# A four-mixer backbone: the closing stage of each layer with the projection kept in PSUM, mask and gate applied apart, block-diagonal scores, one denominator step and folded norm vectors

## The chip, the cores and the metric

The kernel runs on one core of one Trainium2 chip. The metric is device time in microseconds (us) of one execution. Engines are called as in the profile: PE or TensorE (matmul; PEld its weight loads), DVE or VectorE, ACT or ScalarE, POOL or GpSimd, SP or SyncE, which issues all DMAs of this kernel from one queue.

## The reference, cut to what matters

Two layers; 256 context and 2048 latent tokens, width 1024. Each layer projects a normed input, runs four mixers of width 256 (mLSTM, Hyena, GLA, windowed attention), joins their outputs, multiplies by `w_out` and adds the normed, gated result to its input. The change touches the mLSTM's readout, the head norms of mLSTM and GLA, and the joint output projection:

```
# mlstm_chunks, per head
w_intra = exp(d - m);  w_inter = exp(inter - m)          # d is masked to -inf outside the triangle
s   = (q @ k^T) * w_intra
num = w_inter * (q @ c_prev) + s @ v
den = w_inter * (q @ n_prev) + sum(s)
h   = num / max(abs(den), exp(-m))                       # one scan forward, one backward, added
# finish (mLSTM; GLA without the sigmoid)
h = h * sigmoid(o);  h = h * rsqrt(mean_head(h*h) + EPS) * norm_g;  h = h * silu(gate)
# close of the layer
y = concat([a, hyena, gla, attn]) @ w_out[l]
x = x + gt * (y * rsqrt(mean(y*y) + EPS) * g_post)
```

Latent tokens alone are returned, so layer 1 needs no output for the context.

## The kernel before, in words

Tokens are cut into 18 tiles of 128 (2 context, 16 latent). The projections into the mixers run on TensorE as three products of rounded parts (`float32r` high and low), spread between the mixers' own work by marks. The outputs of Hyena, GLA and attention are left, transposed, in the DRAM tensor `aT`.

`tail` (line 1605) closes a layer. It loads `w_out` in 16 blocks of 128x512 through the tile `raw`, a ring of two buffers that all weight loads share: ScalarE rounds a block (`hi`, line 1617), POOL makes the rest (`lo`, line 1618). Then it runs two kinds of generators in turn over the tiles (18 in layer 0, 16 in layer 1), `mlstm_chunk` of tile T and `out_tile` of tile T - 1, with two of them open at a time.

`mlstm_chunk` (line 777) loads the chunk's `aT` part, `qk`, `v`, the states `cb`, the gates `og` and, for each half `m` of two heads, `E`: the row of maxima `m_M` broadcast to 128 partitions. The scores go to the PSUM tile `psA` (two banks), one product of 64 rows for each head (line 801). VectorE subtracts the gate and applies the mask in one instruction for each direction and head (line 804, eight a chunk); ScalarE takes the Exp (line 806); VectorE multiplies with the scores (line 808). `pi` (line 810) is q times the state, `po` (line 816) the weighted values; both stand in PSUM banks `psb` and `psc`. VectorE scales and adds them into `nd` (lines 812, 818), and makes the denominator `r` (lines 821 to 823) and the quotient (line 824) for each half; POOL adds the directions (line 825). `head_norm` (line 657) norms the heads and multiplies by the norm vector `ngb` on POOL (line 665). TensorE transposes the result (line 834, bank `pse`), and it becomes k = 0, 1 of the eight parts of tile T.

`out_tile` (line 1626) rounds the eight parts (line 1638 on ScalarE, line 1639 on POOL) and multiplies them with `w_out` in two halves of 512 columns: 24 matmuls a half (lines 1650 to 1652), k = 2 to 7 first, 0 and 1 last. The sums stand in the PSUM tag `pp`, two banks. VectorE copies a bank to `y` (line 1653), ScalarE squares it in place and sums (line 1654), the small norm steps follow on VectorE and ScalarE, VectorE scales the 1024 columns (line 1659), POOL adds them to `x` (line 1660), and SP stores the tile. In layer 0 six of the tiles are then followed by the input norm of a tile for layer 1 (`norm_tile`, lines 360 to 380, with transposes on TensorE, line 370).

The order of instructions on each engine isn't the order of the code: the framework orders them by a simulated timeline when it builds the program. On the chip each engine runs its list in order, and each tile's buffers tie the engines together by semaphores.

## Time and profile before

| what | us |
|---|---|
| median of 3 runs | 3533.69 |
| lowest, highest | 3526.88, 3543.3 |
| the profiled execution | 3536.89 |
| its span in the profile | 3535.1 |

The profile is of one execution. A time in a timeline counts from the start of its span. Busy time of an engine leaves out its waits on semaphores, but an instruction that is held up after its start counts as busy; matmuls overlap, so the sum of their durations is more than their busy time. The two tails lie at about 1533 to 1883 us (layer 0) and 3228 to 3535 us (layer 1).

### The profile page before, as it was taken

Reading aid. Unit: us, or ns where it says so; the run is one execution under the profiler, and the core shown is the slowest. Engines: PE = TensorE matmul, PEld = TensorE weight load, DVE = VectorE, ACT = ScalarE, POOL = GpSimd, SP = SyncE. Lnnn points to the kernel's source line nnn. Section 1 sums busy time; section 2 is a strip of 40 time slices with the busy share of each in tenths; the row PEclk is TensorE's granted clock in tenths of the full one; section 3 lists DMA queues with packets and bytes.
Section 4 is the critical chain, followed back from the end, with each engine's and each line's share of the span. In section 5 each row is a group of like instructions: output and inputs, shape, how many; then the busy total and the mean of one; then the engine's idle time right before and its main releaser. Section 6 shows DMA issues by size and latency. Waiting matters only on the chain. (4 is left out here: it accounts for less than half of the span.)

```text
span 3535.1 us, 70724 instructions
## 1 busy us (share of the span) xinstructions
PE 3226.2 (91%) x25897; PEld 2653.8 (75%) x25897; DVE 2046.1 (58%) x5374; ACT 1434.5 (41%) x3722; POOL 1153.3 (33%) x1559
## 2 busy tenths in 40 slices
PE   6989999999998988888998899998999999887998
PEld 4778878798886677777777677776888887776776
DVE  6733565553345565568888534656432457745887
ACT  5513444332544444133444323444333546522433
POOL 3711111233123344145555420112231135422555
PEclk8999999999998989989999899999999999998999
DMA  7374443684355532475444365443863443327453
GB/s 248 105 203 125 116 117 101 186 247 130 111 167 155 149 111 82 120 203 176 154 138 137 97 178 156 118 116 118 242 185 97 123 119 105 101 84 210 152 162 106
DMA packets 554861, 508.24 MB, mean 144 GB/s; under 512 B 114896, under 2 KB 484877, under 8 KB 554515
## 3 DMA queue, kind: packets, MB, share of 16 engines
q1 hardware_dynamic: 554515, 503.73, 48.3%
q8 instruction: 205, 3.36, 0.4%
q14 instruction: 141, 1.16, 0.1%
HBM read 337.64 MB, written 165.92 MB: 142 GB/s over the span
## 5 line engine op out<-in xcount | busy, mean ns | idle before, releaser
L480 PE MATMUL pp<-w,hi 128*128 128x256 f32 (+2 forms) x1984 | 602.8, 305 | 23.6 <-ACT w L425 10.4
L482 PE MATMUL pp<-w,hi 128*128 128x256 f32 (+2 forms) x1984 | 595.6, 301 | 4.5 <-POOL w L426 4.5
L483 PE MATMUL pp<-w,ho 128*128 128x256 f32 (+2 forms) x1984 | 590.8, 298 | 5.1 <-POOL ho L380 5.0
L463 PE MATMUL pp<-hi,w 128*128 128x512 f32 (+1 forms) x1328 | 527.0, 397 | 6.5 <-ACT w L425 5.2
L466 PE MATMUL pp<-hi,w 128*128 128x512 f32 (+1 forms) x1328 | 513.6, 389 | 1.2 <-POOL w L426 1.0
L465 PE MATMUL pp<-ho,w 128*128 128x512 f32 (+1 forms) x1328 | 513.6, 387 | 0.0
L480 PEld LDWEIGHTS pp<-w,hi 128*128 128x128 f32 x1984 | 389.3, 197 | 46.4 <-ACT w L425 13.9
L482 PEld LDWEIGHTS pp<-w,hi 128*128 128x128 f32 x1984 | 390.5, 197 | 17.4 <-issue 8.6
L483 PEld LDWEIGHTS pp<-w,ho 128*128 128x128 f32 x1984 | 391.0, 197 | 16.4 <-issue 7.5
L426 POOL TENSOR_TENSOR w<-raw,w 128x256 fp32r<-128x256 f32 (+2 forms) x256 | 194.1, 775 | 554.0 <-ACT w L425 519.2
L463 PEld LDWEIGHTS pp<-hi,w 128*128 128x128 f32 x1328 | 255.9, 193 | 61.0 <-issue 7.3
L466 PEld LDWEIGHTS pp<-hi,w 128*128 128x128 f32 x1328 | 251.8, 191 | 53.2 <-issue 3.9
L465 PEld LDWEIGHTS pp<-ho,w 128*128 128x128 f32 x1328 | 253.6, 191 | 44.1 <-issue 3.0
L1650 PE MATMUL pp<-woh,w 128*128 128x512 f32 x544 | 235.5, 433 | 19.2 <-ACT pp L1654 9.0
L1651 PE MATMUL pp<-wol,w 128*128 128x512 f32 x544 | 223.4, 411 | 0.0
L1652 PE MATMUL pp<-woh,w 128*128 128x512 f32 x544 | 219.2, 412 | 2.0 <-POOL w L1639 2.0
L1010 ACT COPY M<-X 128x512 f32<-128x512 f32 x204 | 128.9, 632 | 181.5 <-DVE X L1034 73.3
L216 DVE COPY st<-pp 128x256 f32<-128x256 f32 (+2 forms) x152 | 79.6, 524 | 205.2 <-PE pp L483 106.1
L218 ACT COPY st<-pp 128x256 f32<-128x256 f32 (+2 forms) x152 | 68.7, 452 | 262.0 <-PE pp L483 140.9
L1032 DVE TENSOR_TENSOR X<-X,A 128x256 f32<-128x256 f32 x204 | 109.4, 536 | 94.8 <-ACT M L1010 92.6
L425 ACT CAST w<-raw 128x256 fp32r<-128x256 f32 (+2 forms) x256 | 96.9, 407 | 158.1 <-DMA raw<-in_w_in_dram 96.7
L1219 POOL TENSOR_TENSOR sg<-sg,gt 128x256 f32<-128x256 f32 x34 | 24.9, 733 | 393.8 <-ACT sg L654 324.8
(589 smaller groups left out, 6932.2 us busy)
## 6 DMA issues: line engine op xcount, KB each, us to landing
raw<-in_w_in_dram SPq DMA_DIRECT2D x96, 256.0 KB
q<-d_tq SPq DMA_DIRECT2D x68, 256.0 KB
E<-d_mM SPq DMA_DIRECT2D x68, 256.0 KB
d_yraw<-st SPq DMA_DIRECT2D x64, 256.0 KB
raw<-in_w_ada_dram SPq DMA_DIRECT2D x64, 256.0 KB
X<-d_gqk SPq DMA_DIRECT2D x102, 128.0 KB
wsho<-d_aT SPq DMA_DIRECT2D x34, 384.0 KB
kl<-d_tk SPq DMA_DIRECT2D x28, 384.0 KB
```

The lines of the kernel that those rows point to most:

```text
L426: nc.gpsimd.tensor_sub(out=t[:, 1, :n], in0=raw[:, i, :n], in1=t[:, 0, :n])
L463: mm = nc.tensor.matmul(out=ps[:, :n], lhsT=a, rhs=hi[:, k], start=(k == 0), stop=False)
L465: nc.tensor.matmul(out=ps[:, :n], lhsT=a, rhs=lo[:, k], start=False, stop=False)
L466: nc.tensor.matmul(out=ps[:, :n], lhsT=b, rhs=hi[:, k], start=False, stop=(k == KD - 1))
L480: mm = nc.tensor.matmul(out=ps[:, :n], lhsT=a, rhs=wk[k][:, 0, :n], start=(k == 0), stop=False)
L482: nc.tensor.matmul(out=ps[:, :n], lhsT=a, rhs=wk[k][:, 1, :n], start=False, stop=False)
L483: nc.tensor.matmul(out=ps[:, :n], lhsT=b, rhs=wk[k][:, 0, :n], start=False, stop=(k == KD - 1))
L1010: nc.scalar.copy(out=grid(M, 0, (cc, 2), (x, 512 // x), (1, cc)), in_=grid(X, 0, (512 + cc, 2), (x, 512 // x), (1, cc)))
L1032: nc.vector.tensor_mul(out=t, in0=t, in1=grid(A, f + 2 * b + 1, (-2 * b - 1, 2), (2, b), (0, cc)))
L1650: nc.tensor.matmul(out=ps, lhsT=ak[k][:, 0], rhs=hi[:, k], start=(k == order[0]), stop=False)
L1651: nc.tensor.matmul(out=ps, lhsT=ak[k][:, 0], rhs=lo[:, k], start=False, stop=False)
L1652: nc.tensor.matmul(out=ps, lhsT=ak[k][:, 1], rhs=hi[:, k], start=False, stop=(k == order[-1]))
```

## The change

- **Projection.** A half's sums stay in their PSUM bank: ScalarE squares out of the bank into `y` as scratch, and VectorE scales straight from the bank after the norm, 512 columns at a time; POOL adds 512 columns at a time. Every third half uses a new bank `psd`, which is free because `psA` now takes one bank.
- **Mask and gate.** VectorE adds the mask to all of `E` (128x512) in one instruction; the gate becomes the bias of the Exp, which therefore runs once for each direction and head.
- **Scores.** One product of 128 rows and 256 columns for a half: `qb` holds q of two heads on the block diagonal, zeros elsewhere (cleared once on POOL, two buffers). It is loaded by two more DMAs a chunk.
- **Denominator.** `nd` holds both halves; `r` is made once a chunk, and POOL adds the directions once.
- **Norm vectors.** `head_norm` no longer multiplies by `ngb`, in mLSTM and in GLA. Instead ScalarE scales the blocks k = 0, 1, 4, 5 of `w_out` by the norm vectors (16 more passes in both layers), which are loaded as columns.

```
--- before.py
+++ after.py
@@ -654,7 +654,7 @@
         nc.scalar.activation(out=s, in_=s, func=ACTF.Exp, scale=-1.0)
         return s
 
-    def head_norm(self, p, h, ngb):
+    def head_norm(self, p, h):
         nc = self.nc
         sq = p.tile([P, 4, 64], F32, tag="so", name="sq", bufs=1)
         ss = p.tile([P, 4], F32, tag="hns", name="ss")
@@ -662,7 +662,6 @@
         nc.vector.reduce_sum(out=ss, in_=sq, axis=AX.X)
         self.rsqrt_mean(p, ss, 64, "hn")
         nc.vector.tensor_mul(out=h, in0=h, in1=ss.unsqueeze(2).to_broadcast([P, 4, 64]))
-        nc.gpsimd.tensor_mul(out=h, in0=h, in1=ngb)
 
     def rounds(self, gens, depth, lead):
         gens = iter(gens)
@@ -767,20 +766,23 @@
                 self.m_S = self.states(p, "m", 65, self.m_qk, self.m_v, weigh, lambda d, c, m: ac[:, d, c, m:m + 1], "cd", (3, 1))
 
     def mlstm_setup(self, l, p):
-        ngb = p.tile([P, 4, 64], F32, name="ngb", bufs=1)
-        self.bcast(ngb.rearrange("p h d -> p (h d)"), self.a["mlstm_norm_g"][l], 256)
         cb = [p.tile([P, 2, 2, 2, 65], F32, name=f"cb{i}", bufs=1) for i in range(2)]
-        for t in cb:
+        qb = [p.tile([P, 2, 2, P], F32, name=f"qb{i}", bufs=1) for i in range(2)]
+        for t in cb + qb:
             self.nc.gpsimd.memset(t, 0.0)
-        return cb, ngb
+        return cb, qb
 
     def mlstm_chunk(self, p, c, shared, ar):
         nc = self.nc
         g, wi, em, ws, ac = self.tabs
-        cbt, ngb = shared[0][c % 2], shared[1]
+        cbt, qbt = shared[0][c % 2], shared[1][c % 2]
         nc.sync.dma_start(out=ar[:, 2:], in_=self.aT[c, :, 2:])
         qk = p.tile([P, 4, P], F32, tag="qk", name="qk")
-        nc.sync.dma_start(out=qk, in_=self.qk_src(self.m_qk, c))
+        src = self.qk_src(self.m_qk, c)
+        nc.sync.dma_start(out=qk, in_=src)
+        for h in range(2):
+            r = slice(64 * h, 64 * h + 64)
+            nc.sync.dma_start(out=qbt[r, :, h], in_=src[r, :2])
         v = p.tile([P, 4, 65], F32, tag="v", name="v")
         nc.sync.dma_start(out=v.rearrange("p h d -> p (h d)"), in_=self.m_v[c])
         for h in range(2):
@@ -792,41 +794,40 @@
         s = self.sigm(p, og, 512, "sg", 2)
         nc.gpsimd.tensor_mul(out=s[:, 256:], in0=s[:, 256:], in1=og[:, 256:])
         yield
-        pS = self.ps("A", (P, 2, 512))
+        pS = self.ps("A", (P, 2, 2, P))
+        nd = p.tile([P, 2, 2, 2, 65], F32, tag="nd", name="nd")
         for m in range(2):
             E = p.tile([P, 2, 2, P], F32, tag="E", name="E", bufs=4)
             nc.sync.dma_start(out=E, in_=self.m_M[c, :, 2 * m:2 * m + 2].rearrange("(o d) h t -> o d h t", o=1).broadcast_to([P, 2, 2, P]))
-            for h in range(2):
-                r = slice(64 * h, 64 * h + 64)
-                nc.tensor.matmul(out=pS[:, h, m * P:m * P + P], lhsT=qk[r, 2 + m], rhs=qk[r, m], start=True, stop=True)
+            nc.tensor.matmul(out=pS[:, m], lhsT=qk[:, 2 + m], rhs=qbt[:, m], start=True, stop=True)
+            nc.vector.tensor_add(out=E, in0=E, in1=self.mbig.unsqueeze(2).to_broadcast([P, 2, 2, P]))
             for d in range(2):
                 for h in range(2):
-                    nc.vector.scalar_tensor_tensor(out=E[:, d, h], in0=E[:, d, h], scalar=g[:, d, c, 2 * m + h:2 * m + h + 1],
-                                                   in1=self.mbig[:, d], op0=ALU.subtract, op1=ALU.max)
-            nc.scalar.activation(out=E, in_=E, func=ACTF.Exp, scale=-1.0)
+                    nc.scalar.activation(out=E[:, d, h], in_=E[:, d, h], func=ACTF.Exp, scale=-1.0, bias=g[:, d, c, 2 * m + h:2 * m + h + 1])
             yield
-            nc.vector.tensor_mul(out=E, in0=E, in1=pS[:, :, m * P:m * P + P].unsqueeze(1).to_broadcast([P, 2, 2, P]))
+            nc.vector.tensor_mul(out=E, in0=E, in1=pS[:, m].unsqueeze(1).to_broadcast([P, 2, 2, P]))
             pi = self.ps(T_I[m], (P, 2, 2, 65))
             nc.tensor.matmul(out=pi, lhsT=qk[:, m], rhs=cbt[:, :, m], start=True, stop=True)
-            nd = p.tile([P, 2, 2, 65], F32, tag="nd", name="nd", bufs=3)
-            nc.vector.tensor_mul(out=nd, in0=pi, in1=wi[:, c, :, 2 * m:2 * m + 2].unsqueeze(3).to_broadcast([P, 2, 2, 65]))
+            nc.vector.tensor_mul(out=nd[:, m], in0=pi, in1=wi[:, c, :, 2 * m:2 * m + 2].unsqueeze(3).to_broadcast([P, 2, 2, 65]))
             po = self.ps(T_O[m], (P, 2, 2, 65))
             for d in range(2):
                 for h in range(2):
                     nc.tensor.matmul(out=po[:, d, h], lhsT=E[:, d, h], rhs=v[:, 2 * m + h], start=True, stop=True)
             yield
-            nc.vector.tensor_add(out=nd, in0=nd, in1=po)
-            r = p.tile([P, 2, 2], F32, tag="r", name="r")
-            den = nd[:, :, :, 64]
-            nc.vector.scalar_tensor_tensor(out=r, in0=den, scalar=-1.0, in1=den, op0=ALU.mult, op1=ALU.max)
-            nc.vector.tensor_max(out=r, in0=r, in1=em[:, c, :, 2 * m:2 * m + 2])
-            nc.vector.reciprocal(out=r, in_=r)
-            nc.vector.tensor_mul(out=nd[:, :, :, :64], in0=nd[:, :, :, :64], in1=r.unsqueeze(3).to_broadcast([P, 2, 2, 64]))
-            nc.gpsimd.tensor_add(out=hh[:, 2 * m:2 * m + 2], in0=nd[:, 0, :, :64], in1=nd[:, 1, :, :64])
+            nc.vector.tensor_add(out=nd[:, m], in0=nd[:, m], in1=po)
             yield
+        r = p.tile([P, 2, 2, 2], F32, tag="r", name="r")
+        den = nd[:, :, :, :, 64]
+        nc.vector.scalar_tensor_tensor(out=r, in0=den, scalar=-1.0, in1=den, op0=ALU.mult, op1=ALU.max)
+        nc.vector.tensor_max(out=r, in0=r, in1=em[:, c].rearrange("p d (m h) -> p m d h", m=2))
+        nc.vector.reciprocal(out=r, in_=r)
+        for m in range(2):
+            nc.vector.tensor_mul(out=nd[:, m, :, :, :64], in0=nd[:, m, :, :, :64], in1=r[:, m].unsqueeze(3).to_broadcast([P, 2, 2, 64]))
+        nc.gpsimd.tensor_add(out=hh.rearrange("p (m h) d -> p m h d", m=2), in0=nd[:, :, 0, :, :64], in1=nd[:, :, 1, :, :64])
+        yield
         hf = hh.rearrange("p h d -> p (h d)")
         nc.vector.tensor_mul(out=hf, in0=hf, in1=s[:, :256])
-        self.head_norm(p, hh, ngb)
+        self.head_norm(p, hh)
         nc.gpsimd.tensor_mul(out=hf, in0=hf, in1=s[:, 256:])
         yield
         ps = self.ps(T_E)
...
     def gla_mix(self, l):
-            ngb = p.tile([P, 4, 64], F32, name="ngb", bufs=1)
-            self.bcast(ngb.rearrange("p h d -> p (h d)"), self.a["gla_norm_g"][l], 256)
...
@@ -1606,6 +1605,9 @@
         nc, a = self.nc, self.a
         last = l == DEPTH - 1
         tiles = list(range(NCT if last else 0, NT))
+        gn = self.gp.tile([P, 4], F32, tag="gn", name="gn")
+        for i, nm in enumerate(("mlstm_norm_g", "gla_norm_g")):
+            nc.sync.dma_start(out=gn[:, 2 * i:2 * i + 2], in_=a[nm][l].rearrange("(k p) -> p k", p=P))
         W = []
         for half in range(2):
             hi = self.hp.tile([P, KD, 512], F32R, tag="hi", name="woh", bufs=4)
@@ -1614,9 +1616,12 @@
             for k in range(KD):
                 raw = self.raw()[:, :, :256]
                 nc.sync.dma_start(out=raw, in_=a["w_out"][l, k * P:(k + 1) * P, 512 * half:512 * half + 512].rearrange("p (i n) -> p i n", i=2))
+                if k in (0, 1, 4, 5):
+                    nc.scalar.activation(out=raw, in_=raw, func=ACTF.Copy, scale=gn[:, (0, 1, 4, 5).index(k):(0, 1, 4, 5).index(k) + 1])
                 nc.scalar.copy(out=hi[:, k].rearrange("p (i n) -> p i n", i=2), in_=raw)
                 nc.gpsimd.tensor_sub(out=lo[:, k].rearrange("p (i n) -> p i n", i=2), in0=raw, in1=hi[:, k].rearrange("p (i n) -> p i n", i=2))
         self.h = {}
+        self.no = 0
         ws = [self.hp.tile([P, 4, D], F32, tag=t, name="ws" + t, bufs=4) for t in ("hi", "ho")]
         with self.banks(f"tl{l}"), self.pool(f"tl{l}") as p:
             shared = self.mlstm_setup(l, p)
@@ -1642,22 +1647,26 @@
                 yield
                 y = ws[0][:, 3]
                 ss = p.tile([P, 2], F32, tag="ss", name="ss")
+                acc = []
                 for half in range(2):
                     hi, lo = W[half]
                     sl = slice(512 * half, 512 * half + 512)
-                    ps = self.psp.tile([P, 512], F32, tag="pp", name="pp")
+                    self.no += 1
+                    ps = self.psp.tile([P, 512], F32, tag="pp", name="pp") if self.no % 3 else self.ps("d")
+                    acc.append(ps)
                     for k in order:
                         nc.tensor.matmul(out=ps, lhsT=ak[k][:, 0], rhs=hi[:, k], start=(k == order[0]), stop=False)
                         nc.tensor.matmul(out=ps, lhsT=ak[k][:, 0], rhs=lo[:, k], start=False, stop=False)
                         nc.tensor.matmul(out=ps, lhsT=ak[k][:, 1], rhs=hi[:, k], start=False, stop=(k == order[-1]))
-                    nc.vector.tensor_copy(out=y[:, sl], in_=ps)
-                    nc.scalar.activation(out=ps, in_=ps, func=ACTF.Square, accum_out=ss[:, half:half + 1])
+                    nc.scalar.activation(out=y[:, sl], in_=ps, func=ACTF.Square, accum_out=ss[:, half:half + 1])
                     yield
                 rs = p.tile([P, 1], F32, tag="rs", name="rs")
                 nc.vector.tensor_add(out=rs, in0=ss[:, 0:1], in1=ss[:, 1:2])
                 self.rsqrt_mean(p, rs, D, "o")
-                nc.vector.scalar_tensor_tensor(out=y, in0=y, scalar=rs, in1=gb, op0=ALU.mult, op1=ALU.mult)
-                nc.gpsimd.tensor_add(out=x, in0=x, in1=y)
+                for half in range(2):
+                    sl = slice(512 * half, 512 * half + 512)
+                    nc.vector.scalar_tensor_tensor(out=y[:, sl], in0=acc[half], scalar=rs, in1=gb[:, sl], op0=ALU.mult, op1=ALU.mult)
+                    nc.gpsimd.tensor_add(out=x[:, sl], in0=x[:, sl], in1=y[:, sl])
                 nc.sync.dma_start(out=dst(T), in_=x)
                 yield
                 if not last and T in NS:
```

How this moves instructions, as built. SP at the start of layer 1's tail, from the first chunk's `qk` on (`cb` and `qb` are the two buffers of each):

```order
L783 DMA qk<-d_mqk 128x4x128
L785 DMA v<-d_mv 128x260
L788 DMA cb_36627<-d_mS 64x4x65 x2
L790 DMA og<-d_mog 128x512
L798 DMA E<-d_mM 128x2x256 x2
L783 DMA qk<-d_mqk 128x4x128
L785 DMA v<-d_mv 128x260
L788 DMA cb_36628<-d_mS 64x4x65 x2
L790 DMA og<-d_mog 128x512
L798 DMA E<-d_mM 128x2x256 x2
```

and with the change:

```order
L782 DMA qk<-d_mqk 128x4x128
L787 DMA v<-d_mv 128x260
L790 DMA cb_36485<-d_mS 64x4x65
L785 DMA qb_36487<-d_mqk 64x2x128 x2
L790 DMA cb_36485<-d_mS 64x4x65
L792 DMA og<-d_mog 128x512
L801 DMA E<-d_mM 128x2x256 x2
L782 DMA qk<-d_mqk 128x4x128
L785 DMA qb_36488<-d_mqk 64x2x128 x2
L787 DMA v<-d_mv 128x260
L790 DMA cb_36486<-d_mS 64x4x65 x2
```

`ngb`, which stood ahead of the first `qk`, is gone; each chunk has its two `qb` loads among its loads, ahead of `og` and `E`. VectorE in layer 1's steady part, over the small norm steps of an output tile (`rs`, 128x1) and those of a chunk (`ss`, 128x4):

```order
L229 TENSOR_TENSOR t<-t,v 128x4
L823 RECIPROCAL r<-r 128x4
L230 SCALAR_TENSOR_TENSOR ss<-t,ss 128x4
L824 TENSOR_TENSOR nd<-nd,r 128x4x64
L804 SCALAR_TENSOR_TENSOR E<-E,G,mbig 128x128
L664 TENSOR_TENSOR hh<-hh,ss 128x256
L804 SCALAR_TENSOR_TENSOR E<-E,G,mbig 128x128 x2
L228 SCALAR_TENSOR_TENSOR t<-rs 128x1
L804 SCALAR_TENSOR_TENSOR E<-E,G,mbig 128x128
L229 TENSOR_TENSOR t<-t,v 128x1
L230 SCALAR_TENSOR_TENSOR rs<-t,rs 128x1
L1659 SCALAR_TENSOR_TENSOR wshi<-wshi,rs 128x1024
```

and with the change:

```order
L225 TENSOR_SCALAR v<-rs 128x1
L664 TENSOR_TENSOR hh<-hh,ss 128x256
L808 TENSOR_TENSOR E<-E,psA 128x512
L228 SCALAR_TENSOR_TENSOR t<-rs 128x1
L229 TENSOR_TENSOR t<-t,v 128x1
L651 TENSOR_SCALAR sg<-og 128x512
L230 SCALAR_TENSOR_TENSOR rs<-t,rs 128x1
L803 TENSOR_TENSOR E<-E,mbig 128x512
L1668 SCALAR_TENSOR_TENSOR wshi<-pp,rs,wshi 128x512
L1668 SCALAR_TENSOR_TENSOR wshi<-psd,rs,wshi 128x512
```

The masking of four blocks is one addition (`E<-E,mbig`), and the scaling of 1024 columns out of `wshi` is two of 512 out of two banks. TensorE in layer 1's steady part, at the scores of a half:

```order
L1652 MATMUL pp<-woh,w 128x512
L816 MATMUL psb<-v,E 128x65 x4
L801 MATMUL psA<-qk 128x128 x2
L1650 MATMUL pp<-woh,w 128x512
L1651 MATMUL pp<-wol,w 128x512
```

and with the change:

```order
L1660 MATMUL pp<-woh,w 128x512
L815 MATMUL psb<-v,E 128x65 x4
L802 MATMUL psA<-qb_36488,qk 128x256
L1658 MATMUL psd<-woh,w 128x512
L1659 MATMUL psd<-wol,w 128x512
```

The scores of a half were two products (one for each head) and are one of twice the columns; the output matmuls behind them, which all went to `pp`, go to `psd` for every third half.

## Rows read from the trace of the kernel before

**Rows 1.** Page: busy us of each engine (share of span), instructions.
```profile
PE 3226.2 (91%) x25897; PEld 2653.8 (75%) x25897; DVE 2046.1 (58%) x5374; ACT 1434.5 (41%) x3722; POOL 1153.3 (33%) x1559
```

**Rows 2.** Stretches: length, busy us (instructions) by engine, clock, DMA share, GB/s.
```profile
1533.00:1580.00 47.00, 38.43 (x166) 29.38 (x165) 37.55 (x110) 17.97 (x38) 18.58 (x25) 0.73 0.81 241
1580.00:1883.00 303.00, 276.05 (x1294) 218.74 (x1293) 259.06 (x637) 118.09 (x327) 170.99 (x184) 0.93 0.46 144
3228.00:3285.00 57.00, 40.79 (x164) 30.73 (x163) 31.16 (x105) 14.52 (x30) 15.55 (x25) 0.64 0.69 173
3285.00:3510.00 225.00, 212.93 (x1041) 167.44 (x1040) 194.14 (x490) 86.80 (x232) 125.54 (x149) 0.98 0.49 150
```

**Rows 3.** Waits of TensorE, layer 0, 1580 to 1883: us in total, times, longest.
```profile
PE pp L1650 <- ACT pp L1654: 5.8, 5, 2.5
PE pp L1650 <- ACT w L1638: 5.3, 3, 2.6
PE psb L810 <- DVE nd L818: 5.0, 2, 4.1
PE psc L810 <- DMA cb<-d_mS: 3.0, 1, 3.0
```

**Rows 4.** By line, same stretch: names, shapes, count; busy us, mean ns; idle before.
```profile
L804 DVE SCALAR_TENSOR_TENSOR E<-E,G,mbig 128x128 f32<-128x128 f32 x104 | 44.9, 481 | 3.2 <-DMA E<-d_mM 3.2
...
L1659 DVE SCALAR_TENSOR_TENSOR wshi<-wshi,rs 128x1024 f32<-128x1024 f32 x17 | 24.6, 1450 | 0.4
L1653 DVE COPY wshi<-pp 128x512 f32<-128x512 f32 x34 | 23.0, 681 | 5.7 <-PE pp L1652 3.1 <-POOL wshi L1660 2.3 <-POOL w L426 0.3
...
L808 DVE TENSOR_TENSOR E<-E,psA 128x512 f32<-128x512 f32 x29 | 19.6, 677 | 1.8 <-PE psA L801 1.8
L1654 ACT ACTIVATE pp<-pp 128x512 f32<-128x512 f32 x33 | 19.2, 582 | 44.0 <-DVE wshi L1653 43.9
L821 DVE SCALAR_TENSOR_TENSOR r<-nd 128x4 f32<-128x4 f32 x30 | 17.3, 576 | 0.1
...
L806 ACT ACTIVATE E<-E 128x512 f32<-128x512 f32 x26 | 16.4, 632 | 52.8 <-DVE E L804 45.6 <-issue 2.3 <-PE pp L1652 1.9
```

**Rows 5.** Waits of TensorE, layer 1, 3285 to 3510.
```profile
PE psb L816 <- DVE E L808: 6.6, 7, 1.8
```

**Rows 6.** Timeline, VectorE, layer 1's filling: start us, us, names, count [idle before].
```profile
3263.20 1.14 DVE L804 SCALAR_TENSOR_TENSOR E<-E,G,mbig 128x128 f32<-128x128 f32 x4 [1.71 <-DMA E<-d_mM]
```

**Rows 7.** Timeline of ScalarE, ahead of layer 1's tail.
```profile
3163.69 0.42 ACT L646 ACTIVATE G<-t 128x72 f32<-128x72 f32 x2
```

**Rows 8.** Timeline near the end: a tile's last matmuls, and its scaling.
```profile
3510.75 0.39 PE L1651 MATMUL pp<-wol,w 128*128 128x512 f32 x1
...
3510.98 0.40 PE L1652 MATMUL pp<-woh,w 128*128 128x512 f32 x1
...
3515.07 1.85 DVE L1659 SCALAR_TENSOR_TENSOR wshi<-wshi,rs 128x1024 f32<-128x1024 f32 x1
```

**Rows 9.** Timeline of TensorE, layer 1's steady part: state products and scores.
```profile
3453.42 0.60 PE L810 MATMUL psb<-cb,qk 128*128 128x260 f32 x2
...
3459.26 0.49 PE L801 MATMUL psA<-qk 64*128 64x128 f32 x4
```

**Rows 10.** Timelines, ScalarE, POOL, SP issues: staging of w_out; a chunk's first load.
```profile
3194.34 0.62 ACT L1617 CAST woh<-raw 128x512 fp32r<-128x512 f32 x1 [2.14 <-DMA raw<-in_w_out_dram]
...
3195.04 1.27 POOL L1618 TENSOR_TENSOR wol<-raw,woh 128x512 fp32r<-128x512 f32 x1 [1.75 <-ACT woh L1617]
...
3196.33 0.37 SPq L1616 DMA_DIRECT2D raw<-in_w_out_dram  x1
...
3240.61 0.57 SPq L783 DMA_DIRECT2D qk<-d_mqk  x1
```

**Rows 11.** Timelines, ScalarE, VectorE, layer 0: Square and scaling of one tile.
```profile
1609.02 0.58 ACT L1654 ACTIVATE pp<-pp 128x512 f32<-128x512 f32 x1 [3.01 <-DVE wshi L1653]
...
1616.24 1.74 DVE L1659 SCALAR_TENSOR_TENSOR wshi<-wshi,rs 128x1024 f32<-128x1024 f32 x1
```

83 lines of the change are left out of this document (46 added, 37 removed).

## The prediction

> **What bounds the kernel now.** I read the page first: TensorE is busy 91% of the span and VectorE 58% [rows 1], so VectorE as a whole bounds nothing. The change is almost all inside `tail`, which runs twice, and an average over the span says nothing about it. So next I cut both tails into a filling part, in which the mLSTM chunks run with hardly any projection beside them, and a steady part, in which one chunk and one output tile pass per turn [rows 2]. In the steady parts VectorE is busy 259 of 303 us (layer 0) and 194 of 225 us (layer 1), 85% and 86%, and TensorE 276 and 213. So TensorE is still the engine nearest to full. It loses two things: idle time, 303 - 276 = 27 us and 225 - 213 = 12 us, and clock. The granted clock is 0.93 and 0.98 there, so 0.07 x 276 = 19 us and 0.02 x 213 = 4 us are lost to stretches at 1.2 instead of 2.4 GHz; in the filling parts it is 0.73 and 0.64. Idle and clock together are 62 us, and no relief of another engine can give back more than that in these stretches.
>
> Then I read what TensorE waits for there. In layer 0 the largest wait is for a projection bank (5.8 us), then a transposed and cast chunk (5.3), then VectorE's `nd` (5.0), then a DMA (3.0) [rows 3]. The bank comes late because ScalarE's Square waits for VectorE's copy out of the same bank: 43.9 of the 44.0 us that ScalarE sat idle before line 1654 are put down to line 1653 [rows 4]. In layer 1 the largest wait is for VectorE's `E` product, 6.6 us [rows 5]. Named directly, VectorE ends 5.8 + 5.0 + 6.6 = 17 of the 39 us idle, 45%. The 5.3 us end with a chain (head norm, transpose, copy, cast) that has VectorE steps in it too.
>
> **The change part by part: VectorE in the steady parts.** I count layer 0, stretch 1580 to 1883 [rows 4]. Removed: the masking instructions of line 804, 44.9 us for 104; the two copies a tile, 23.0 us for 34; the 1024-wide scaling of line 1659, 24.6 us for 17; half of the denominator instructions, of which I count line 821 alone, 17.3 / 2 = 8.7 us. Sum 101 us. Added: 26 additions of 128x512 (104 / 4) and 34 scalings of 128x512 out of PSUM. Line 808 is the nearest row for both, 512 columns, one operand in PSUM, 677 ns. For the scalings I take it: 34 x 0.677 = 23 us. The additions have both operands in SBUF, like line 804, and line 804 is stretched: 481 ns on average, against 1.14 / 4 = 285 ns where nothing else ran [rows 6], a factor 1.7. So an addition costs 0.68 to 1.14 us, 18 to 30 us in all. Relief: 101 - 23 - (18 to 30) = 48 to 60 us of 259; VectorE falls from 85% to some 67%. These are sums of durations that overlap a little, so an estimate. Layer 1 has 11 chunks in its stretch where layer 0 has 13: some 40 to 51 of 194.
>
> What of this reaches the end is bounded by the 62 us above. The releasers name VectorE for 45%; with a part of the cast chain I take a half, 31 us. The low end is 10 (the in-order queues then wait for the next thing, `E`'s DMA above all), the high end 55 (all but the DMA wait and some clock).
>
> **ScalarE.** Eight Exps of 128 columns replace two of 512. The nearest rows: two of 72 columns take 0.42 us [rows 7], one of 512 columns 632 ns [rows 4]. So an Exp of 128 columns lies between 0.21 and 0.63 us, nearest to the first; along the line between them it is 0.21 + 56 x 0.42 / 440 = 0.26. That makes 8 x 0.26 = 2.1 against 1.3 us, 0.8 us more a chunk. ScalarE is busy 118 of 303 us, 39% [rows 2]; it hides this. Without that cover it is 34 chunks x 0.8 = 27 us.
>
> **The bank that is held.** A projection bank is now freed only after Square, norm and scaling; in return there are three banks. In layer 1, where little stands in the queues, the last matmul of a tile starts at 3510.98 and the scaling at 3515.07 [rows 8]. Without the copy (0.68) and with the first scaling (0.68) the first bank is free 4.1 us after that matmul starts. The new order of TensorE puts at least 18 projection matmuls (the first half of the next tile) and a group of mLSTM matmuls in front of the first matmul that needs that bank: 18 x 0.23 (spacing in [rows 8]) = 4.1, plus 0.5 for the scores [rows 9] and as much again for the rest, so 5 us at the least, but for the last tile, and about 7 in the middle. Cost taken: nothing. If the cover is gone, see the second rival.
>
> **Scores on TensorE.** Four instructions on 64 rows (two heads) become two on 128 rows, 256 columns, with zeros in the other head's half. The four take 0.49 us; two instructions on 128 rows with 260 columns take 0.60 [rows 9]. So a chunk half costs 0 to 0.11 us more; 68 of them, 0 to 7 us; I take 0, since the columns streamed are equal (2 x 128). The four 64-row instructions follow each other; nothing shows two of them at once. The Trainium skill says otherwise ("TensorE: Matmul & The Clock Gate", Part 3: Packing small matmuls): products on different row groups overlap in the array. If they had, the pair would have cost about a half and this edit would add 68 x 0.25 = 17 us, for a sum of 3527; since the row prices the pair as it runs here, I give that no chance.
>
> **The filling parts.** Each chunk has two more loads on SP's queue, and `qb` must be cleared by POOL first. SP spends 0.57 us on such an issue there [rows 10], so before the second chunk's `E` loads stand four more, 2.2 us, less the norm vector's load that goes. Behind them on SP are the chunk's `v`, `cb`, `og` and `E`, and VectorE waits for `E` in just this place (1.71 us, [rows 6]). VectorE's shorter masking gives some of it back. I take +2 us a layer, +4; ends -3 and +6.
>
> **The staging of w_out.** Eight of sixteen blocks a layer get one more ScalarE pass of 0.62 us (that of the cast, [rows 10]) in a ring of two buffers. A load of `raw` goes out at 3196.33, just after POOL released the buffer at 3195.04 + 1.27 = 3196.31 [rows 10]: the ring paces SP, and the loads of the state updates stand behind it. Four passes a buffer make 4 x 0.62 = 2.5 us a layer; I take +2, +4 in all, ends 0 and +6. The norm vectors' own small loads come earlier and are hidden.
>
> **The rest.** The last tile saves a copy (0.68) and half a scaling before its store: -1 us. POOL loses 34 products of 256 columns in the GLA mix, and the scheduler reorders other stages too; taken as 0, within 5 us either way.
>
> **Sum.** 3536.9 (profiled execution) - 31 + 4 + 4 - 1 = 3512.9. That execution was 3.2 us above the median 3533.7, so 3509.7, rounded 3510 us.
>
> **The rivals.** First: VectorE was not what held TensorE. For it speaks that TensorE is busy 91 and 95% of the steady parts, that VectorE itself waits for `E`'s DMA [rows 4, 6], and that the first wait it stops ending will be ended by that DMA or by the cast chain. Then nothing comes back and the costs stay: 3533.7 + 7 = 3541 us, no change.
>
> Second, the one on the slow side: the held bank. In layer 0, where the norm of the next layer's tiles stands in the same queues, Square started at 1609.02 and the scaling at 1616.24 [rows 11], 7.2 us; with 0.4 for the last matmul and 0.68 for the scaling the bank would come free after 8.3 us, against a cover of 5 to 8. If most of layer 0's 18 tiles look so, each waits some 1.5 us, and some 1 us more goes to the low clock that follows idle time: 18 x 2.5 = 45 us, 3510 + 45 = 3555 us. It decides as soon as the chain from Square to scaling is above some 7 us on average. Against it: the copy leaves the chain and VectorE's queue gets a fifth shorter.
>
> Third: the whole of it comes back, idle and clock, because each wait that goes also saves a low-clock stretch behind it: 3510 - 24 = 3486 us.
>
> **How the numbers follow.** The forecast has 0.50 (its own range 3496 to 3524), no gain 0.22 (3530 to 3545), the held bank 0.13 (3550 and above), the full gain 0.15 (3480 to 3496). A range of 8 in 10 leaves out the held bank and the edge of the full gain: 3484 to 3545. About 0.5%, 17.7 us, can be told from no change, so faster means below 3516: three quarters of the forecast and the full gain, 0.53; slower the held bank, 0.13; the same 0.34.
>
> **What would show it.** Steady parts of some 285 and 217 us in place of 303 and 225, VectorE under 70% busy there, a granted clock of 0.96 or more in layer 0. The wait for the bank now ends in VectorE's scaling; over 10 us in total for it would prove the second rival. If TensorE's idle time stays at 39 us with VectorE at 67%, the first rival is right. Filling parts longer by over 6 us, or a stretch from the first `w_out` load to the first chunk longer by over 6, would show that I priced the loads too low. I would be wrong altogether if stages outside both tails moved by more than 10 us through the scheduler's new order.

## The result and the profile after

The changed kernel takes 3486.7 us (median; 3483.8 to 3488.9) beside 3535.7 of the kernel before on the same chip: a ratio of 0.986, interval 0.984 to 0.989, so 49 us faster. The forecast was 3510, range 3484 to 3545. Page of after, busy us of each engine, share of the span, instructions (as [rows 1]):

```profile
PE 3193.5 (92%) x25761; PEld 2638.8 (76%) x25761; DVE 1926.2 (55%) x5034; ACT 1473.6 (42%) x3942; POOL 1102.1 (32%) x1495
```

From here on one cut serves for all kernels: *filling* is from the start of the first output matmul to the start of the Square of tile 0's second half, *steady* from there to the start of the last output matmul, and both together are a *tail*. Before, filling and steady take 45.2 and 302.8 us in layer 0, 56.5 and 239.0 in layer 1 (the prediction's cut ended layer 1 at 3510). Views by stretch, first before (steady parts alone), then after (filling, steady, filling, steady); columns as in [rows 2]:

```profile
1579.00:1882.00 303.00, 276.69 (x1296) 219.54 (x1294) 259.03 (x639) 118.40 (x328) 170.14 (x183) 0.93 0.46 144
3285.00:3524.00 239.00, 225.41 (x1094) 177.00 (x1093) 199.73 (x505) 89.66 (x242) 130.31 (x153) 0.99 0.47 145
```

```profile
1545.00:1587.00 42.00, 34.85 (x134) 26.16 (x133) 25.02 (x60) 21.67 (x59) 16.84 (x19) 0.72 0.90 265
1587.00:1865.00 278.00, 256.88 (x1252) 209.13 (x1251) 208.89 (x507) 134.88 (x420) 159.16 (x175) 0.99 0.54 168
3198.00:3252.00 54.00, 42.76 (x139) 31.94 (x140) 27.65 (x68) 20.37 (x60) 12.34 (x18) 0.62 0.66 176
3252.00:3475.00 223.00, 215.99 (x1045) 176.84 (x1045) 151.28 (x383) 99.76 (x309) 120.46 (x141) 1.00 0.52 161
```

VectorE falls from 259 to 209 us in layer 0 and from 200 to 151 in layer 1, and the granted clock of layer 0 rises from 0.93 to 0.99. The tails shrink from 348.0 + 295.5 = 643.5 us to 319.4 + 277.2 = 596.6: 47 of the 49 us. The rest moved both ways: 1534 to 1545 us up to the first output matmul, 1347 to 1333 between the tails.

What TensorE waits for in the steady parts of after, layer 0 and then layer 1 (us in total, times, longest; as [rows 3, 5]):

```profile
PE pp L1658 <- DVE wshi L1668: 5.9, 4, 2.5
PE psb L810 <- DVE nd L817: 4.2, 4, 2.0
PE psm L370 <- DVE wsho L364: 2.7, 2, 1.5
PE psd L1658 <- DVE wshi L1668: 2.7, 3, 1.3
```

```profile
PE pp L1658 <- ACT w L1643: 2.4, 2, 1.4
PE pp L1658 <- DVE wshi L1668: 2.1, 3, 1.3
PE psd L1658 <- DVE wshi L1668: 0.8, 1, 0.8
```

The wait for a bank now ends in VectorE's scaling, 8.6 us in layer 0 and 2.9 in layer 1. The wait for the `E` product, 6.6 us in layer 1 before, is gone. By line, layer 0 of after from 1586 to 1865 us (as [rows 4]):

```profile
L806 ACT ACTIVATE E<-E,G 128x128 f32<-128x128 f32 x113 | 36.7, 390 | 57.3 <-DVE E L803 50.5 <-DVE v L225 4.1 <-PE psc L815 2.5
L803 DVE TENSOR_TENSOR E<-E,mbig 128x512 f32<-128x512 f32 x28 | 23.4, 837 | 12.8 <-DMA E<-d_mM 12.7
L1668 DVE SCALAR_TENSOR_TENSOR wshi<-pp,rs,wshi 128x512 f32<-128x512 f32 x23 | 16.6, 744 | 0.2
L1661 ACT ACTIVATE wshi<-pp 128x512 f32<-128x512 f32 x24 | 14.1, 587 | 12.2 <-PE pp L1660 12.2
```

Square out of `pp` waits for TensorE now, not for VectorE. One tile in layer 1, whose first half stands in `psd` and whose second in `pp`, shows the held bank at work; timelines of ScalarE (Square of the second half), VectorE (the two scalings) and TensorE (the next matmul into `psd`):

```profile
3407.23 0.58 ACT L1661 ACTIVATE wshi<-pp 128x512 f32<-128x512 f32 x1
3410.92 0.74 DVE L1668 SCALAR_TENSOR_TENSOR wshi<-psd,rs,wshi 128x512 f32<-128x512 f32 x1
3411.58 0.74 DVE L1668 SCALAR_TENSOR_TENSOR wshi<-pp,rs,wshi 128x512 f32<-128x512 f32 x1
3411.72 0.50 PE L1658 MATMUL psd<-woh,w 128*128 128x512 f32 x1
```

From this Square to the second bank's release it takes 5.1 us, and to the first scaling 3.7. Over the 34 tiles of both layers the way from that Square to the first scaling averages 4.2 us and is above 7 in two (from all starts in the trace). `psd` is free at 3411.66, and TensorE writes it at 3411.72: in this tile the third bank carried it over the chain with nothing to spare.

### The profile page after: what moved, and what is told of

It reads as the page before. It is cut to its first block, busy times and chain, and to the rows that moved or that the text cites. A ratio compares the mean times of both kernels' runs of the same rounds, so it can differ in the third digit from the quotient of the medians.

```text
span 3484.7 us, 70453 instructions
## 1 busy us (share of the span) xinstructions
PE 3193.5 (92%) x25761; PEld 2638.8 (76%) x25761; DVE 1926.2 (55%) x5034; ACT 1473.6 (42%) x3942; POOL 1102.1 (32%) x1495
## 5 line engine op out<-in xcount | busy, mean ns | idle before, releaser
L482 PEld LDWEIGHTS pp<-w,hi 128*128 128x128 f32 x1984 | 388.8, 196 | 15.2 <-issue 8.1
L1658 PE MATMUL pp<-woh,w 128*128 128x512 f32 x368 | 154.8, 421 | 14.5 <-DVE wshi L1668 8.0
L806 ACT ACTIVATE E<-E,G 128x128 f32<-128x128 f32 x272 | 88.0, 390 | 143.2 <-DVE E L803 110.2
L1659 PE MATMUL pp<-wol,w 128*128 128x512 f32 x368 | 147.3, 401 | 0.8 <-POOL wol L1622 0.8
```

The costliest lines, as they stand in the source:

```text
L482: nc.tensor.matmul(out=ps[:, :n], lhsT=a, rhs=wk[k][:, 1, :n], start=False, stop=False)
L1658: nc.tensor.matmul(out=ps, lhsT=ak[k][:, 0], rhs=hi[:, k], start=(k == order[0]), stop=False)
L1659: nc.tensor.matmul(out=ps, lhsT=ak[k][:, 0], rhs=lo[:, k], start=False, stop=False)
```

## The experiments

All kernels ran beside the kernel before. Tails are from each kernel's profile, ratios from its timed runs.

| kernel | tails, us | VectorE, steady, layer 0 / 1 | clock | ratio to before (interval) |
|---|---|---|---|---|
| before | 643 | 85 / 84% | 0.93 / 0.99 | 1 |
| changed | 597 | 75 / 68% | 0.99 / 1.00 | 0.986 (0.984 to 0.989) |
| changed, again | 594 | 75 / 67% | 0.98 / 0.99 | 0.984 (0.981 to 0.987) |
| fold alone | 651 | 87 / 80% | 0.94 / 0.93 | 1.006 (1.005 to 1.008) |
| late loads | 612 | 77 / 66% | 0.98 / 1.00 | 0.997 (0.995 to 0.999) |
| copy restored | 617 | 81 / 75% | 0.97 / 0.98 | 0.993 (0.991 to 0.994) |
| mask restored | 597 | 82 / 77% | 0.99 / 0.99 | 0.992 (0.991 to 0.994) |
| loads between | 596 | 75 / 66% | 0.97 / 0.99 | 0.986 (0.984 to 0.989) |
| two banks | 684 | 60 / 57% | 0.92 / 0.95 | 1.015 (1.013 to 1.018) |
| denominators by halves | 591 | 80 / 69% | 0.99 / 1.00 | 0.988 (0.987 to 0.990) |
| copy and two banks | 622 | 80 / 73% | 0.95 / 0.95 | 0.993 (0.991 to 0.995) |
| scores and third bank alone | 652 | 85 / 84% | 0.93 / 0.97 | 1.000 (0.999 to 1.001) |
| no fold | 610 | 78 / 71% | 0.99 / 0.99 | 0.992 (0.991 to 0.994) |
| kept projection and third bank alone | 607 | 86 / 81% | 0.99 / 0.99 | 0.990 (0.988 to 0.992) |

**The fold alone, on the kernel before.** Edit: `head_norm` without `ngb`, in mLSTM and GLA, and the scaling of `w_out` by `gn`.

> The kernel before with the folded norm vectors alone: no multiplication by the norm vector in the mLSTM and GLA heads, and w_out scaled instead. In the built order the two small loads of the norm vectors (gn) for layer 0 now stand at the start of the program, since nothing holds them back, and the order of every engine differs from before from the first microseconds on. Theory 'order': all of the 11 us that the changed kernel loses before its first output matmul (1534 to 1545 us) comes from this part. Then this kernel's first output matmul comes at about 1545 too, with the first matmul of the attention projection near 294 us in place of 274, its layer-0 GLA mix is about 13 us shorter, its steady parts stay near 309 and 242 us, and its time is 3535 +- 12 us. Rival 'chance': the 11 us differ from execution to execution and have nothing to do with the change: the first output matmul comes at 1534 +- 5 us and the attention projection starts near 274.

3550.8 us, slower by 0.6%; first output matmul at 1537 us, which is in the range of the rival and not at the 1545 of the other theory; steady parts 300 and 249. Neither theory gave the loss: layer 1's steady part is 10 us longer, its clock 0.93 in place of 0.99, with as much idle time of TensorE as before (13.8 against 13.6 us).

**The loads of `gn` late.**

```
-        gn = self.gp.tile([P, 4], F32, tag="gn", name="gn")
+        with self.pool(f"gn{l}", 1) as pn:
+            gn = pn.tile([P, 4], F32, name="gn")
```

> The changed kernel with one thing else: the tile of the norm columns comes from a pool that opens with the closing stage, so the two small loads can't be put at the start of the program. Up to the GLA mix of layer 0 every engine's order is then that of the kernel before. Theory 'order': the attention projection starts near 274 us again, the 11 us before the first output matmul and up to 13 more (the GLA mix without its norm vector) come back, and the kernel takes 3465 to 3480 us against 3487 of the changed one. Rival 'late loads': the small loads now stand in SP's queue right ahead of w_out, whose scaling waits for them, and the state updates behind; then the staging of w_out is some 3 to 10 us longer in each layer and the time is 3480 to 3500.

First output matmul at 1534 us, as expected, but the kernel takes 3517.7, above the ranges of both theories. Between the tails it takes 1356 us (1333 and 1341 in two profiles of the changed kernel), which neither theory has. The pool closes behind the staging of `w_out`, which now starts 40 us ahead of the first output matmul in both layers, in place of 50 and 60, and its end is exposed: layer 0's filling takes 59.5 us in place of 41.3. ScalarE in layer 1 waits for the blocks; two of these waits:

```profile
3199.17 1.31 ACT L1622 CAST woh<-raw 128x512 fp32r<-128x512 f32 x2 [5.95 <-DMA raw<-in_w_out_dram]
3204.06 0.72 ACT L1621 ACTIVATE raw<-raw,gn 128x512 f32<-128x512 f32 x1 [3.58 <-DMA raw<-in_w_out_dram]
```

**The copy restored, three banks kept.**

```
+                    nc.vector.tensor_copy(out=y[:, sl], in_=ps)
-                    nc.scalar.activation(out=y[:, sl], in_=ps, func=ACTF.Square, accum_out=ss[:, half:half + 1])
+                    nc.scalar.activation(out=ps, in_=ps, func=ACTF.Square, accum_out=ss[:, half:half + 1])
...
+                nc.vector.scalar_tensor_tensor(out=y, in0=y, scalar=rs, in1=gb, op0=ALU.mult, op1=ALU.mult)
+                nc.gpsimd.tensor_add(out=x, in0=x, in1=y)
```

> The changed kernel with the copy out of the bank restored (VectorE copies each half, ScalarE squares in place, one scaling of 1024 columns and one POOL addition), but with the third bank kept. VectorE gets about 23.5 us more in the steady part of layer 0 and 20 in layer 1. Theory 'relief' (the gain follows the VectorE time that a part takes away; about 120 us of it went and 48.5 us came back in the steady parts, 0.4 us each): 44 x 0.4 = 18 us slower than the changed kernel, 3505, split about evenly over the layers, and TensorE's wait for banks as now. Rival 'bank chain' (the copy mattered because it stood between the matmuls and Square, so that the bank came late): 25 us or more slower, with TensorE's wait for a projection bank back to 8 us or more in layer 0. Rival 'slack' (VectorE at 75% has room): within 5 us of 3487.

3503.7 us; steady parts 18.1 us longer together (286.5 + 232.6 against 278.1 + 222.9). The size is that of the relief theory; the runs below show that VectorE's time as such doesn't give it.

**The fused mask restored.** Edit: lines 804 and 806 of before in place of the addition and the four Exps.

> The changed kernel with the fused mask and gate restored (eight VectorE instructions of 128 columns and two Exps a chunk). VectorE gets about 22 us more in layer 0's steady part (45 to 47 against 23.4) and 28 more in layer 1's (47.3 against 18.9); ScalarE gets 19 and 15 us less. Theory 'relief': 50 x 0.4 = 20 us slower, 3507, somewhat more of it in layer 1. Rival 'slack': within 5 us, since the addition and four Exps make E no earlier than four masks and one Exp did: about 0.84 + 4 x 0.39 = 2.4 us against 4 x 0.48 + 0.63 = 2.55. Rival 'Exp': faster by over 5 us, because ScalarE's eight short Exps are in the way of Square and the casts.

The tails are what they were, 597 us, with VectorE at 82% in layer 0 in place of 75:

```profile
1591.00:1862.00 271.00, 254.65 (x1217) 203.99 (x1217) 223.24 (x572) 116.63 (x328) 153.84 (x170) 0.99 0.54 168
```

The relief theory falls for the tails: 37 us more of VectorE's time in the steady parts (223 against 209, 174 against 151) cost them nothing. ScalarE has 30 us less to do there (117 against 135, 88 against 100), so this run by itself doesn't tell VectorE's share from ScalarE's; the denominators below add VectorE time without that, and cost nothing either. The kernel is still slower than the changed one, 3503.7, which is close to the 3507 of the relief theory, but by luck: its stages between the tails take 1358 us, in an order that differs from the changed kernel's from about the 20th matmul there. Why that order is worse wasn't tried.

**The changed kernel again.**

> The changed kernel, unaltered, once more with its own profile. Question: do the lengths of its stages differ from execution to execution, or with the built order? Read so far: before the first output matmul 1534 us (before), 1545 (changed), 1543 and 1543 (two kernels with the changed order there), 1534 (a kernel with the order of before there); between the tails 1347 (before), 1333 (changed), 1358 (changed with the old masking). Theory 'order': this execution has 1545, 278, 1333 and 223 us (up to the first output matmul, steady part of layer 0, between the tails, steady part of layer 1) within 3 us each, and a time within 5 us of 3487. Rival 'chance': one of them is off by over 8 us.

1537.7, 277.9, 1341.0 and 223.0 us, where the first profile had 1545.2, 278.1, 1333.3 and 222.9. The steady parts repeat within 0.2 us; the stages outside the tails move by 7.5 and 7.7 us with the same order, over the 3 us of the one theory and just under the 8 of the other. So the 11 and 14 us of the first profile are partly chance.

**The loads of `gn` in between.** Edit: the tile of `gn` and its loads stand ahead of `gla_proj`.

> The changed kernel with the two small loads of the norm columns neither at the start of the program (as in the changed kernel) nor right ahead of w_out's scaling (as in the run with the late loads, where the first output tile came 18 us later in layer 0 and the second tail started 26 us later), but in between: their tile comes from a pool that opens with the GLA projection. Up to the GLA mix the order is that of the kernel before. Theory 'order': the first output matmul comes at 1534 +- 3 us in place of 1545, the filling parts stay at 41 and 54 us, and the time is 3470 to 3480 us, unless the stages between the tails fall into another order (1333 to 1358 us seen so far), which may give back up to 25 us. Rival: the 11 us come from something else in the fold (w_out's scaling); then the first output matmul stays at 1543 to 1545.

First output matmul at 1526 us, tails 596, but 1350 between them: 3483.9 us, the same ratio as the changed kernel. Six profiles with the order of before up to the GLA mix have that matmul at 1526 to 1534 us (mean 1530.6), eight with the changed order at 1537 to 1545 (mean 1540.2). So two loads of a KB, put near the program's start because nothing held them back, came with some 10 us more up to that matmul through the order. SP issues them there:

```profile
35.01 0.38 SPq L1610 DMA_DIRECT2D gn<-in_mlstm_norm_g_dram  x1
```

**Two banks for the kept projection.**

```
-                    ps = self.psp.tile([P, 512], F32, tag="pp", name="pp") if self.no % 3 else self.ps("d")
+                    ps = self.psp.tile([P, 512], F32, tag="pp", name="pp")
```

> The changed kernel with two projection banks, as before, in place of three; nothing else. A bank is then freed only after Square, norm and scaling, with no third one to cover. Theory 'held bank': the cover of the first bank shrinks by the 24 matmuls of one half, 24 x 0.23 = 5.6 us, to some 1 to 3 us, against a chain from the last matmul to the scaling of 4 to 8 us; TensorE waits 2 us or more for a bank on each of 33 tiles, mostly ending in VectorE's scaling, and the time is 3550 us or more. Rival 'filled': the built order puts a chunk's matmuls there, TensorE waits under 1 us a tile more, and the time is below 3510.

3587.0 us, 1.5% slower than before, and the tails 88 us longer than with three banks, though VectorE is at 60%. Steady parts, and TensorE's largest wait in layer 0:

```profile
1578.00:1910.00 332.00, 288.80 (x1253) 224.69 (x1254) 200.10 (x507) 139.76 (x421) 163.12 (x178) 0.92 0.45 141
3301.00:3562.00 261.00, 234.68 (x1045) 184.17 (x1045) 149.47 (x385) 100.11 (x310) 120.41 (x142) 0.95 0.44 139
```

```profile
PE pp L1658 <- DVE wshi L1668: 19.5, 9, 3.5
```

This is the second rival, in its pure form: 43.6 us idle and a clock of 0.92 in layer 0.

**Denominators by halves.** Edit: lines 821 to 825 of before, for each half.

> The changed kernel with the denominator made for each half again (two short chains and two POOL additions a chunk). VectorE gets about 13 us more in layer 0's steady part and as much in layer 1's (30.1 and 31.1 before for the three short steps, 13.4 and 14.4 now, less 3.5 us for the longer quotients). Restoring the copy cost 18 us in the steady parts for 44 us of VectorE (0.4 each); restoring the mask cost nothing there for 50. Theory 'relief': 26 x 0.4 = 10 us slower in the steady parts, 5 a layer. Rival 'chain': the quotient is made earlier by halves, so the head norm and the transposes come earlier, and the steady parts are shorter by 3 us or more. Rival 'slack': within 3 us.

3490.2 us, tails 591, steady parts 273.1 + 230.4, within 3 us of the changed kernel's sum, with 16 us more of VectorE's time in them. The single chain is worth nothing that can be told.

**Copy and two banks.** Edit: both of the above together.

> The changed kernel with the copy restored and with two projection banks: neither the kept projection nor the third bank, all other parts as changed. The two tails (first to last output matmul, both layers together) took 643 us before, 597 and 594 changed, 617 with the copy and three banks, 684 with the kept projection and two banks; 597 with the old masking, 591 with the old denominators. So mask and denominators gave nothing. Theory 'third bank' (the gain comes from the third bank and, on top of it, from dropping the copy): without both the tails are back at 635 to 650 us, and the time is 3525 to 3545. Rival 'other parts' (scores, or the parts that gave nothing alone but do together): the tails are at 615 to 625 us, the time at 3500 to 3515, as with the copy and three banks.

Tails 622, 3508.4 us. The third bank is worth 6 us where there is a copy, and mask, denominators, scores and fold together 21 beside the kernel before (643 to 622). The theory that only banks matter falls.

**Scores and third bank alone, on the kernel before.** Edit: `qb`, one product for a half, `psA` in one bank, `self.ps("d")` for every third half.

> The kernel before with block-diagonal scores, which free a bank, and that bank as a third one for the projection; copy, mask, denominators and norm vectors as before. Theory 'third bank': the tails shrink from 643 to 615 to 625 us (as in the changed kernel with the copy restored, which has the same banks), and the time is 3505 to 3517 us, though VectorE is as busy as before. Rival 'relief' (without less work on VectorE a third bank only moves the wait): the tails stay within 8 us of 643.

3531.8 us, no change; tails 652, 9 us more, where the one theory had 615 to 625 and the rival at most 8 either way. With a copy and a full VectorE a third bank and the scores that free it give nothing; what each of the two is worth isn't told apart.

**No fold.** Edit: `ngb` back in both mixers, `w_out` unscaled, denominators by halves.

> The changed kernel without the folded norm vectors (POOL multiplies by them in the mLSTM and GLA heads again, w_out isn't scaled) and with the denominators by halves, which makes room for the norm vector's tile; kept projection, three banks, mask and scores as changed. Alone on the kernel before the fold cost 22 us. Theory 'fold costs': up to the first output matmul the order is that of before, 1526 to 1534 us in place of 1538 to 1545, the filling parts lose w_out's extra passes, and POOL's extra product stays hidden: tails 580 to 592 us, time 3465 to 3478, faster than the changed kernel. Rival 'POOL in the chain': the product by the norm vector (0.94 us, then the gate's) lengthens the chain from the head norm to the transposes, on which the last two of eight parts of each output tile depend; tails of 600 us or more and a time of 3490 or more.

3505.8 us, tails 610. The rival has the time, but not the reason: TensorE's largest waits in its tails are for `nd` (11.4 us, layer 0) and for the loads of `qb` (7.4 us, layer 1), not for POOL. So the fold costs 8 us of tail on the kernel before and saves 19 here (610 against 591, the kernel with denominators by halves). 17 of the 19 lie in the filling parts (51.1 + 53.7 against 41.9 + 46.0), where the wait for the first `qb` in layer 1 is 7.4 us without the fold and 2.5 with it. Why the sign turns stays open.

**Kept projection and third bank alone, on the kernel before.** Edit: as in the run with scores and third bank, and the copy dropped.

> The kernel before with two parts of the change, block-diagonal scores with the third bank they free, and the projection kept in PSUM; mask, denominators and norm vectors as before. Tails so far: 643 us before, 652 with scores and third bank alone, 622 with every part but kept projection and third bank, 595 changed, 597 changed with the old masking, 610 changed without the fold. Theory 'kept bank' (kept projection and third bank carry the gain together, and less work on VectorE is then not needed): tails 595 to 612 us, and a time of 3485 to 3508. Rival 'relief' (VectorE, 85% busy in the steady parts before, must be relieved by mask and denominators too, since the scaling now waits in its queue): tails of 625 us or more and a time of 3515 or more.

3493.4 us, tails 607, as the theory of the kept bank had it: 36 of the 48 us, with VectorE as busy as before. With that other run it makes a pair that differs in the copy (and the scaling by halves) alone, and 45 us of tail (652 to 607). Scores and third bank with the copy, then without it, layers 0 and 1:

```profile
1582.00:1880.00 298.00, 266.25 (x1220) 214.11 (x1220) 254.75 (x625) 117.04 (x325) 165.98 (x183) 0.93 0.49 151
3267.00:3513.00 246.00, 223.38 (x1039) 180.56 (x1038) 207.75 (x505) 87.78 (x242) 136.43 (x153) 0.97 0.48 147
```

```profile
1577.00:1851.00 274.00, 253.63 (x1222) 205.03 (x1221) 235.53 (x614) 115.50 (x327) 168.45 (x201) 0.99 0.52 166
3244.00:3474.00 230.00, 220.55 (x1060) 180.74 (x1059) 185.98 (x497) 89.04 (x245) 133.39 (x171) 0.99 0.51 159
```

The Squares of layer 0 with the copy, and without it (busy, mean ns; idle ahead, and what ended it):

```profile
L1659 ACT ACTIVATE pp<-pp 128x512 f32<-128x512 f32 x22 | 12.8, 581 | 22.0 <-DVE wshi L1658 22.0
L1659 ACT ACTIVATE psd<-psd 128x512 f32<-128x512 f32 x11 | 6.4, 581 | 9.6 <-DVE wshi L1658 9.5
```

```profile
L1660 ACT ACTIVATE wshi<-pp 128x512 f32<-128x512 f32 x22 | 12.8, 583 | 0.0
L1660 ACT ACTIVATE wshi<-psd 128x512 f32<-128x512 f32 x11 | 6.5, 588 | 5.0 <-POOL wshi L1668 4.5 <-POOL sq L661 0.5
```

ScalarE stood still for 31.5 us ahead of its Squares because the copy was in VectorE's queue; without the copy it stands for 5. The casts and Exps that TensorE needs are queued behind those Squares. TensorE's largest waits in layer 1, with the copy, then without it:

```profile
PE pp L1655 <- ACT w L1642: 6.6, 5, 2.3
PE psd L1655 <- ACT w L1642: 4.9, 2, 2.8
```

```profile
PE psd L1657 <- DVE wshi L1667: 4.4, 4, 2.0
PE pp L1657 <- DVE wshi L1667: 3.0, 4, 1.2
```

So 11.5 us of waits for ScalarE's casts are gone in layer 1, against 7.4 for the held bank. In layer 0 the waits that go end in VectorE's `nd` and `E` (10.6 and 5.4 us with the copy, 0.7 and 0.3 without), against 12.1 for the held bank; that those too come by way of ScalarE's Exps is argued from the queue, not shown.

**What they say together.** Most of the gain is the kept projection with a third bank to pay for it. Either without the other gives nothing or a loss (652, 684 us). The other parts give 21 us of tail while the copy is there (643 to 622), relief of VectorE among them; once Square no longer waits for VectorE, 37 us more on that engine change nothing. Alone the two groups give 36 and 21 us, together 48; that they share one wait is what the rows suggest, though no run takes that wait away by itself. Put in order, six of the kernels are a ladder, each with one group of parts more than the one ahead of it: 643 us of tails before, 652 with scores and third bank, 607 with the kept projection, 610 with the mask (no fold), 591 with the fold (denominators by halves), 597 and 594 with the single denominator. So the second step that counts is the fold, and neither the mask nor the denominator; the ratios of the two kernels around it are 0.992 and 0.988.

## Why the prediction was right or wrong

**Right:** the sign, the range, and TensorE as the bound. The result lies 3 us inside the range's low end, outside the forecast's own 3496 to 3524 and in the part that had a chance of 0.15. Idle and clock in the steady parts were 61.5 us on the new cut (26.3 + 0.07 x 277 and 13.6 + 0.01 x 225) and are 30.7 (21.1 + 0.01 x 257 and 7.0 + 0): the half that was forecast. The clock of 0.96 or more came. VectorE's relief of 48 to 60 us in layer 0 was 50, which says nothing of what it was worth. An addition takes 0.84 us (0.68 to 1.14 given), a scaling 0.74 (0.68).

**Wrong in size, the steady term:** 41 us (24.7 + 16.1), not 31. The ten more lie outside the pot of idle time and clock, which I took for all that could come back; the 62 us themselves weren't exceeded. In layer 1 the 716 output matmuls with the gaps behind them took 188.8 us before and 173.6 after (from all starts in the trace), 15.2 less, of which idle (6.6) and clock (2.3) explain 9 at most. A pair of output matmuls usually starts 0.233 us apart. Outside the stretches at 1.2 GHz 69 pairs took over 0.25 us before and 50 after, which is 3.4 us less over the usual step, and neither idle time nor clock. In layer 0 such pairs cost 2.9 us more after, so they don't explain the ten; where those lie stays open.

**Wrong, the scores:** taken as 0, range 0 to 7. By line in layer 1's steady part, before and after:

```profile
L801 PE MATMUL psA<-qk 64*128 64x128 f32 x96 | 11.8, 322 | 0.0
```

```profile
L802 PE MATMUL psA<-qb,qk 128*128 128x256 f32 x48 | 15.2, 398 | 0.0
```

24 halves took 0.49 us each, and take 0.63: 68 x 0.14 = 10 us more on TensorE by these durations; no run changes the scores alone. The reason that I gave is wrong too. The four 64-row instructions are two pairs, and in all 24 halves the two of a pair (one for each head, I infer; the trace doesn't name the rows) start 0.007 us apart, where two instructions of 128 columns on 128 rows (line 834) start 0.108 apart. So they overlap. The Trainium skill ("TensorE: Matmul & The Clock Gate", Part 3: Packing small matmuls) says that products on different rows of the array run at once, and I gave it no chance. In the starts the trace agrees. The price of 17 that I put beside it was too high and mine too low: the second pair starts only 0.214 us after the first, as late as two instructions of 0.107 in a row would put it.

**Wrong, the filling parts:** 4 us more forecast, 6 less on the new cut (45.2 to 41.3 and 56.5 to 54.2; 40.5 and 52.5 in the second profile). But that cut ends with a Square, which waited for the copy before: 5.9 and 3.0 us from the start of tile 0's last output matmul to it, 0.7 and 0.6 after. Up to that matmul the parts hardly moved, 39.3 to 40.7 us and 53.5 to 53.6 (40.1 and 50.2 in the second profile), so the 6 us are the Square's wait and no shorter filling. TensorE waits 3.3 us for `qb` in layer 1's filling:

```profile
PE psA L802 <- DMA qb<-d_mqk: 3.3, 1, 3.3
```

Before, the first chunk's `qk` held it up for 6.7 us in the same place, so the two more loads don't show as a cost. VectorE's work falls from some 37 us [rows 2] to 25.0 in layer 0; what that is worth isn't shown.

**Wrong, the staging of `w_out`:** +4 forecast, next to nothing seen. A scaling pass takes 0.72 us (0.62 assumed), but the last cast in layer 1 still starts 12 us ahead of the first output matmul (13 before). In layer 0 it starts 10.3 us behind that matmul, 1.9 before, and TensorE waits 0.8 us for a block there. The late loads show what the cover is worth. An Exp of 128 columns takes 0.39 us, not 0.26; at 49% in layer 0 ScalarE hides it, as said.

**The reason given for the main term was wrong.** I let the gain follow VectorE's load, and named all its parts as relief. The 45% of idle time that I called VectorE's by name held the 5.8 us for a bank, which [rows 3] put down to ScalarE; by name VectorE has 11.6 of 39 us, 30%. The mask, the largest of them, is worth nothing in the changed kernel's tails, and kept projection and third bank bring 36 us with VectorE at 86% in layer 0. The fold, which I took for 4 us of cost, saves 19 us of tail behind them. So that the sum's main term came out near is in part luck. The row that told it was there: ScalarE's 43.9 us ahead of Square [rows 4]. I used it for the bank alone and not for what else queues on ScalarE.

**The rivals.** The time is the third rival's, 3486, but by luck: half of idle and clock is still there, and its price was wrong, since the 24 us are the way to the high end of 55, where the whole pot of 62 would have given 31 and 3479. The second rival has its chain (4.2 us from Square to scaling on average, above 7 in two tiles of 34, where 7 on average was the point of decision) and even its sign, 11.5 us of bank waits against "over 10"; that mark was badly set, since TensorE was faster all the same. With two banks it decides, and costs 100 us. The first rival is out: the steady parts are 41 us shorter. Stages outside the tails did move by over 10 us in the first profile, by the prediction's own mark a sign of being wrong altogether; up to 8 of that is chance between executions, and the two moves (11 more, 14 less) nearly cancel.

## What to carry to other kernels

Before counting an engine's load, look at who waits in its queue: an instruction that makes a second engine wait (here a copy ahead of a Square) delays all that is queued on that second engine, and taking it out can be worth much though neither engine is the bottleneck (45 us of tail here). Keeping a result in PSUM until a norm is known lengthens the bank's hold; here it needed one bank more in the same edit, and either half alone would have been dropped as useless. A load without a dependency goes wherever the framework likes; look where it went.

## What the runs showed of the hardware

Two matmuls of 64 rows start 7 ns apart, where two of 128 rows and as many columns start 108 ns apart; one product with zeros in their place takes 0.14 us a half more here, and its use is the bank that it frees. Two executions of one program agree within 0.2 us in steady parts of 278 and 223 us, but differ by 8 us in the 1540 us ahead and by 8 us the other way in the 1340 between. Idle time can be paid twice: with two banks, 22 us more idle in layer 0 came with a clock of 0.92 in place of 0.99, which is 0.07 x 289 = 20 us more. But the sum of idle time doesn't set the clock: with the fold alone layer 1 has 13.8 us idle at 0.93, before 13.6 at 0.99, and two executions of the changed kernel have 21.1 us idle at 0.99 and 17.1 at 0.98 in the same 278 us.
